# The output product of a state-space branch: weights split on GpSimd, all eight units in three passes, and a norm placed between its matmuls

## The chip, the cores and the metric

The kernel runs on one core of one Trainium2 chip. A core has five engines, each with its own instruction order: TensorE (PE, matmuls; PEld is its weight load), VectorE (DVE), ScalarE (ACT), GpSimd (POOL) and SyncE (SP, which here issues all loads). They share the on-chip memory SBUF; matmuls write to the banks of PSUM, which GpSimd does not read in this kernel. The metric is the device time of one execution in microseconds, lower is better.

## The reference

Two transformer-like blocks over 256 tokens of width 1024. The change lies in the first one:

```
v   = silu(layer_norm(causal_dwconv(a * sigmoid(g), 31 taps)))   # convolution branch
y_a = v @ w_conv_out
y_b = ssd_branch(...) ; its end:  yn @ w_ssm_out                  # state-space branch, yn 256 x 2048
mix = (sigmoid(gate_a) * y_a + sigmoid(gate_b) * y_b) @ w_o
```

Everything is fp32. Behind the block come a feed-forward layer and a second block with two kinds of attention and 32 experts of which all weights (201 MB) are read.

## The kernel before

**Units and passes.** Weights come in units of 128 x 2048 floats (1 MB, one load each) into a ring of five slots. A unit can be multiplied in two ways. In `MODES` with 4, it goes to TensorE as fp32 (two records per matmul in the trace). Otherwise it is split into a high part `wh` (ScalarE copies it to a rounded type, line 260) and a low part `wl` (what is missing, a subtraction on VectorE, line 261), the activation likewise, and three rounded matmuls per block replace the fp32 one: high x high, high x low, low x high. The split goes by halves of 128x1024; four slots hold `wh` and four `wl`, so a half can be split when TensorE has done with the half four before it.

**Around the change.** `ynT` is the state-space branch's normalised result, channels on partitions; `w_ssm_out` comes in eight units `ws0` to `ws7` of 128 output channels each, and two units share a PSUM bank. `ws0` to `ws3` go in fp32, `ws4` to `ws7` in three passes, with their low parts made on VectorE. `gate_gb` takes the product, scaled, from each bank (line 798).

**The convolution branch** is computed on VectorE by taps (line 665): `cacc = vpad * weight + cacc` on 128x256, 30 for each of eight channel blocks after a first multiplication (line 663). 60 of them and ten more, with two first ones, are still to do when `ws0` starts. Then comes the layer norm over channels: `pair_cs` sums blocks in pairs on VectorE; TensorE sums over partitions by a matmul with ones (`cs`, line 820); VectorE centres (line 823); ScalarE squares into `vpad` (line 825); `pair_cq` and `cq` (line 831) sum the squares; `crs` is the reciprocal root, of which the power is a GpSimd operation (line 249); `crr` (line 836) spreads it to all partitions; VectorE multiplies (line 840), ScalarE applies silu and the parts `cT_ah` and `cT_al` feed the next product with `w_conv_out` (`wc0` to `wc3`, `ps_wc`).

**The order.** The program is written in one order, and a planner with its own costs for each instruction decides how the instructions of different steps stand on each engine; `tc.issue_after(x)` holds back a step until `x` stands in the order. On the chip each engine follows its own order and waits on semaphores.

GpSimd's work before is small: eight multiplications `xh` (line 708) in the state-space core, and the powers.

Of the kernel before, what the change touches and what calls it, by code (L numbers as in the profile page):

```python
# [11 lines left out]
F32 = mybir.dt.float32  # L12
# [4 lines left out]
AF = mybir.ActivationFunctionType  # L17
ALU = mybir.AluOpType
# [16 lines left out]
LN_EPS = 1e-5  # L35
# [154 lines left out]
def block_kernel(ctx, tc, I, out, modes):  # L190
    nc = tc.nc
    V, S, G, PE = nc.vector, nc.scalar, nc.gpsimd, nc.tensor
# [4 lines left out]
    mm = ctx.enter_context(tc.tile_pool(name="mm", bufs=4, space=PSUM))  # L197
    sm = ctx.enter_context(tc.tile_pool(name="sm", bufs=2, space=PSUM))
# [9 lines left out]
    def bank(pool, name):  # L208
        return pool.tile([P, 512], F32, tag="b", name=name)
# [17 lines left out]
    ident = const.tile([P, P], F32, name="ident")  # L227
# [4 lines left out]
    def par(name, i=0, n=1):  # L232
        second, o = PPO[name]
        return (pp2 if second else pp)[:, o + i:o + i + n]

    def row(name, pool):
# [2 lines left out]
        nc.sync.dma_start(r, I["rows"][i:i + 1, :].to_broadcast([P, D]))  # L239
        return r  # L240

    def rsqrt(out, in_, scale, eps):

        n = out.free_size()
        first = V.tensor_scalar(out, in_, scale, eps, op0=ALU.mult, op1=ALU.add).ins
        e = neghalf[:, :n]
        if len(out.shape) == 3:
            e = e.rearrange("p (a b) -> p a b", a=out.shape[1])
        G.tensor_tensor(out, out, e, op=ALU.pow)
        return first  # L250


# [3 lines left out]
    sg_pool = dense.enter_context(tc.tile_pool(name="sg", bufs=2, reuse_waits="tile"))  # L256
    ada_pool = sg_pool

    def split(h, l, f):
        a = S.activation(h, f, AF.Copy)  # L260
        return a.ins, V.tensor_tensor(l, f, h.bitcast(F32), op=ALU.subtract).ins  # L261

    def split_act(a, kt, step=4):
        for k in range(0, kt, step):
# [3 lines left out]
    def act(pool, kt, name, tags=("ah", "al"), f=None):  # L268

        return Act(f, *(pool.tile([P, kt, T], F32R, tag=t, name=f"{name}_{t}") for t in tags))  # L270

    def passes(w, name):

        if name in ready:
            return ready.pop(name)[1]
        kt, n = w.shape[1], w.shape[2]
        if mode_of(name) == 4:
            return [(range(kt), range(n), [("f", w)])]
        if kt * n <= HALF:
            cuts = [(range(kt), range(n))]  # L280
        elif "_" in name or n == P:
            cuts = [(range(k, k + kt // 2), range(n)) for k in (0, kt // 2)]
        else:
            cuts = [(range(kt), range(c, c + n // 2)) for c in (0, n // 2)]
        got = []
        for i, (ks, cs) in enumerate(cuts):
            h, l = (hl.tile([P, HALF], F32R, tag=t, name=f"{t}_{name}_{i}")[:, :len(ks) * len(cs)]
                    .rearrange("p (k n) -> p k n", k=len(ks)) for t in ("wh", "wl"))
            split(h, l, w[:, ks[0]:ks[-1] + 1, cs[0]:cs[-1] + 1])
            got.append((ks, cs, [("h", h), ("l", h), ("h", l)]))  # L290
        return got

# [15 lines left out]
        w, _ = stream(name)  # L308
        ready[name] = (w, passes(w, name))

    def gemm_chan(names, x, pool=mm):

        c, banks = 0, []
        for name in names:
            w, _ = stream(name)
            ps_ = passes(w, name)
            for i in range(w.shape[2] // P):
                if c % 2 == 0:
                    banks.append(bank(pool, f"ps_{name}_{i}").rearrange("p (c t) -> p c t", c=2))
                o = banks[-1][:, c % 2, :]  # L320
                c += 1
                m = order(ps_, i * P, P)
                for j, (k, part, wp) in enumerate(m):
                    PE.matmul(o, wp, getattr(x, part)[:, k, :],  # L324
                              start=(j == 0), stop=(j == len(m) - 1))
        return banks

    def gemm_tok(name, x, ktot, pool=mm, early=0):
# [199 lines left out]
    with ExitStack() as e1:  # L528
        b1 = e1.enter_context(tc.tile_pool(name="b1", bufs=1, reuse_waits="tile"))
        hT = act(b1, 8, "hT")  # L530
        vpad = b1.tile([P, 8, T + CK - 1], F32, tag="vpad", name="vpad")
        cacc = b1.tile([P, 8, T], F32, tag="cacc", name="cacc")
        ynT = Act(b1.tile([P, 16, T], F32, tag="ynT", name="ynT"))
        gate = {n: b1.tile([P, 8, T], F32, name=f"gate_{n}") for n in ("ga", "gb")}
# [5 lines left out]
        with tc.tile_pool(name="pre", bufs=1, reuse_waits="tile") as pre:  # L540
# [60 lines left out]
            m = [(k, w, x) for k in range(8) for w, x in ((wd[0], hT.h), (wd[0], hT.l), (wd[1], hT.h))]  # L601
# [29 lines left out]
            for i in range(2):  # L631
                q = rs[:, RSO[f"lambda_q{i + 1}_2"]:RSO[f"lambda_q{i + 1}_2"] + 64]
                k = rs[:, RSO[f"lambda_k{i + 1}_2"]:RSO[f"lambda_k{i + 1}_2"] + 64]
# [156 lines left out]
        late = e1.enter_context(tc.tile_pool(name="late", bufs=1, reuse_waits="tile"))  # L790
# [4 lines left out]
        def ssm_out(j):
            (ps_,) = gemm_chan([f"ws{2 * j}", f"ws{2 * j + 1}"], ynT)
            gt = gate["gb"][:, 2 * j:2 * j + 2, :]
            V.scalar_tensor_tensor(gt, gt, 1.0, ps_, op0=ALU.add, op1=ALU.mult)

        for j in range(WSJ):  # L800
            ssm_out(j)
        for j in range(0, 8, 2):
            for k in range(CK):
                for i in (j, j + 1):
# [12 lines left out]
        pair = pair_sums(cacc, "cs")
        b = bank(sm, "cs")
        for i in range(2):
            PE.matmul(b[:, :T], ones, pair[:, i, :], start=(i == 0), stop=(i == 1))  # L820
        csq = vpad[:, :, :T]
        for i in range(0, 8, 2):
            V.scalar_tensor_tensor(cacc[:, i:i + 2, :], b[:, None, :T].to_broadcast(both), -1.0 / D, cacc[:, i:i + 2, :],
                                   op0=ALU.mult, op1=ALU.add)
            S.activation(csq[:, i:i + 2, :], cacc[:, i:i + 2, :], AF.Square)

        pair = pair_sums(csq, "cq")
        b = bank(sm, "cq")
        for t in range(2):
            for i in range(2):  # L830
                PE.matmul(b[:, t:t + 1], pair[:, i, t * P:(t + 1) * P], ones[:, 0:1], start=(i == 0), stop=(i == 1))
        crs = late.tile([P, 2], F32, name="crs")
        rsqrt(crs, b[:, 0:2], 1.0 / D, LN_EPS)
        b = bank(sm, "crr")
        for t in range(2):
            PE.matmul(b[:, t * P:(t + 1) * P], crs[:, t:t + 1].to_broadcast([P, P]), ident, start=True, stop=True)
        rrow = b[:, None, :T].to_broadcast(both)
        cT = act(b1, 8, "cT", f=cacc)
        for i in range(0, 8, 2):
            V.tensor_tensor(cacc[:, i:i + 2, :], cacc[:, i:i + 2, :], rrow, op=ALU.mult)  # L840
            for c in range(i, i + 2):
                S.activation(cacc[:, c, :], cacc[:, c, :], AF.Silu, scale=par("conv_ln_g", c), bias=par("conv_ln_b", c))
            cT.last = split(cT.h[:, i:i + 2], cT.l[:, i:i + 2], cacc[:, i:i + 2])[1]
        for j in range(WSJ, 4):
            ssm_out(j)
# [4 lines left out]
        mixhl = b1.tile([P, 16, T], F32R, tag="ynT", name="mixhl")  # L850
        mixT = Act(gate["ga"], mixhl[:, :8], mixhl[:, 8:])
        for j in range(4):
            (ps_,) = gemm_chan([f"wc{j}"], cT)
            gt = gate["ga"][:, 2 * j:2 * j + 2, :]
            V.scalar_tensor_tensor(gt, gt, 1.0, ps_, op0=ALU.add, op1=ALU.mult)
            V.tensor_tensor(gt, gt, gate["gb"][:, 2 * j:2 * j + 2, :], op=ALU.add)
            split(mixT.h[:, 2 * j:2 * j + 2], mixT.l[:, 2 * j:2 * j + 2], gt)
        for n in range(2):
            with tc.issue_after(cT.last):
                end = ada_v(n)  # L860
            for t, ps_ in enumerate(gemm_tok(f"wo{n}", mixT, 8, early=2 * n)):
                o = res[:, t, n * 512:(n + 1) * 512]
# [6 lines left out]
    with ExitStack() as e2:  # L869
        b2 = e2.enter_context(tc.tile_pool(name="b2", bufs=1, reuse_waits="tile"))  # L870
        xn1 = b2.tile([P, 2, D], F32, tag="xn1", name="xn1")
        first, last = (norm_rows(xn1, res, t, "ln1", "ln", 4 * LN_EPS) for t in range(2))
# [14 lines left out]
        for j in range(11):  # L887
            banks = gemm_chan([f"up{j}a0", f"up{j}g0"], h1T)
# [49 lines left out]
    with ExitStack() as e3:  # L938
# [7 lines left out]
        ones = dcon.tile([P, P], F32, name="ones2")  # L946
# [121 lines left out]
        for i in range(4):  # L1068
# [458 lines left out]

WSJ = 1  # L1530
# [15 lines left out]
```

## Time and profile before

| | |
|---|---|
| median of 3 runs | 1241.27 us (1239.9 to 2015.82) |
| the profiled execution | 1243.86 us, its span 1242.2 us |
| busy: TensorE, VectorE | 1201.1 us (97%), 776.2 us (62%) |
| busy: ScalarE, GpSimd | 495.3 us (40%), 26.1 us (2%) |
| moved by loads | 353.03 MB, 284 GB/s on average |

A share of busy time is a mean over stages with different limits. A matmul record is longer than its place in the pipe (consecutive ones overlap), so for TensorE the distances between starts count, not the durations.

### The profile page before, as it was taken

The numbers are of one execution on the slowest core, as the hardware profiler recorded it, in microseconds if no ns is written. First come the engines' busy times: TensorE is split into PE (matmuls) and PEld (weight loads), VectorE is DVE, ScalarE is ACT, GpSimd is POOL, SyncE is SP. The second block draws the span as 40 slices with busy tenths as digits, with TensorE's granted clock in tenths as the row PEclk, the third lists the DMA queues.
The fourth block names the chain that finished last, engine by engine and source line by source line (L and its number), as shares of the span: only waits on it lengthen the run. The fifth ranks groups of instructions, "written<-read, shape, count | busy, mean of one in ns | idle before, by whom it ended". The sixth has DMA issues, their size and how long they took to land. (4 is left out here: it accounts for less than half of the span.)

```text
span 1242.2 us, 19480 instructions
## 1 busy us (share of the span) xinstructions
PE 1201.1 (97%) x7885; PEld 881.1 (71%) x7885; DVE 776.2 (62%) x1515; ACT 495.3 (40%) x823; POOL 26.1 (2%) x39
## 2 busy tenths in 40 slices
PE   7999999999999999999999999999999999999886
PEld 6988998998969999875888898554444454444342
DVE  7999999999868989568777656523222223222222
ACT  6456778744426666434445544311111111111111
POOL 0000100100000000001000000000000000000000
PEclk9999999999999999999999989999999999999999
DMA  9635333235867656755883357899999999999995
GB/s 364 234 137 203 128 145 137 103 105 200 355 260 266 237 199 223 274 209 186 331 351 135 104 193 317 328 410 418 419 419 419 420 419 419 419 419 419 418 418 207
DMA packets 51917, 353.03 MB, mean 284 GB/s; under 512 B 6000, under 2 KB 6640, under 8 KB 10224
## 3 DMA queue, kind: packets, MB, share of 16 engines
q1 hardware_dynamic: 51824, 351.75, 72.2%
q8 instruction: 63, 1.03, 0.3%
q14 instruction: 30, 0.25, 0.1%
HBM read 350.68 MB, written 1.05 MB: 283 GB/s over the span
## 5 line engine op out<-in xcount | busy, mean ns | idle before, releaser
L1435 DVE TENSOR_TENSOR hid<-hid,pu 128x256 f32<-128x256 f32 x32 | 12.0, 418 | 195.3 <-PE pu L1427 195.3
L1427 PE MATMUL pu<-we,xg 128*64 128x512 f32 x512 | 117.3, 593 | 6.4 <-DMA we<-in_experts 6.4
L1483 PE MATMUL pd<-we,hdT 128*64 128x512 f32 x512 | 114.0, 595 | 3.8 <-issue 2.6
L1427 PE MATMUL pg<-we,xg 128*64 128x512 f32 x512 | 114.5, 593 | 0.0
L665 DVE SCALAR_TENSOR_TENSOR cacc<-vpad,pp,cacc 128x256 f32<-128x256 f32 x240 | 101.4, 478 | 0.0
L1427 PEld LDWEIGHTS pu<-we,xg 128*64 128x64 f32 x512 | 37.8, 137 | 82.3 <-issue 68.2
L1427 PEld LDWEIGHTS pg<-we,xg 128*64 128x64 f32 x512 | 38.8, 137 | 72.4 <-issue 67.8
L1483 PEld LDWEIGHTS pd<-we,hdT 128*64 128x64 f32 x512 | 35.5, 137 | 70.9 <-issue 68.9
L260 ACT ACTIVATE osb<-ob 128x512 fp32r<-128x512 f32 x31 | 19.6, 631 | 123.4 <-DVE ob L1487 123.4
L1447 ACT ACTIVATE hdT<-ht 128x512 f32<-128x512 f32 x16 | 9.6, 597 | 148.0 <-PE ht L1446 148.0
L1251 DVE TENSOR_SCALAR xg<-xg,s,mod 128x128 f32<-128x128 f32 x64 | 22.0, 404 | 63.7 <-PE xg L1229 63.7
L1487 DVE SCALAR_TENSOR_TENSOR ob<-pd,wpl,g 128x512 f32<-128x512 f32 x31 | 23.3, 751 | 40.3 <-PE pd L1483 37.7
L1430 ACT ACTIVATE hid<-pg 128x512 f32<-128x512 f32 x16 | 9.6, 597 | 84.0 <-PE pg L1427 84.0
L488 DVE SCALAR_TENSOR_TENSOR sb_ada<-w_ada,silu_c,sb_ada 128x512 f32<-128x512 f32 x49 | 36.6, 747 | 0.6
L261 DVE TENSOR_TENSOR wl_dn<-w_dn,wh_dn 128x1024 fp32r<-128x1024 f32 x21 | 25.7, 1224 | 16.6 <-ACT wh_dn L260 16.4
L1229 PE MATMUL xg<-oh,res 128*128 128x128 bf16 (+1 forms) x512 | 35.4, 222 | 0.0
L261 DVE TENSOR_TENSOR obl<-ob,osb 128x512 fp32r<-128x512 f32 x31 | 21.5, 693 | 21.6 <-ACT osb L260 21.6
L260 ACT ACTIVATE wh_dn<-w_dn 128x1024 fp32r<-128x1024 f32 x21 | 22.3, 1061 | 31.5 <-PE ps_dn L335 27.6
L335 PE MATMUL ps_dn<-wh_dn,guT_gh 128*128 128x512 f32 x84 | 33.7, 401 | 0.0
L335 PE MATMUL ps_dn<-wh_dn,guT_gl 128*128 128x512 f32 x84 | 33.2, 395 | 0.0
L324 PE MATMUL ps_xs<-hT_al,wh_xs 128*128 128x256 f32 x128 | 32.2, 287 | 0.0
L324 PE MATMUL ps_xs<-hT_ah,wh_xs 128*128 128x256 f32 x128 | 31.4, 281 | 0.0
(853 smaller groups left out, 3209.9 us busy)
## 6 DMA issues: line engine op xcount, KB each, us to landing
we<-in_experts SPq DMA_DIRECT2D x189, 1024.0 KB, 19.9
w_ada<-in_stream SPq DMA_DIRECT2D x22, 1024.0 KB, 6.4
w_dn<-in_stream SPq DMA_DIRECT2D x10, 1024.0 KB, 4.9
w_xs<-in_stream SPq DMA_DIRECT2D x8, 1024.0 KB, 4.8
w_z<-in_stream SPq DMA_DIRECT2D x8, 1024.0 KB, 4.8
w_ws<-in_stream SPq DMA_DIRECT2D x8, 1024.0 KB, 4.8
w_bc<-in_stream SPq DMA_DIRECT2D x4, 1024.0 KB, 4.8
w_ga<-in_stream SPq DMA_DIRECT2D x4, 1024.0 KB, 5.0
```

The source lines that it names most:

```text
L260: a = S.activation(h, f, AF.Copy)
L261: return a.ins, V.tensor_tensor(l, f, h.bitcast(F32), op=ALU.subtract).ins
L324: PE.matmul(o, wp, getattr(x, part)[:, k, :], start=(j == 0), stop=(j == len(m) - 1))
L335: PE.matmul(banks[t], getattr(x, p_)[:, u + k, t * P:(t + 1) * P], wp, start=(u == 0 and j == 0), stop=(u + kt == ktot and j == len(m) - 1))
L488: V.scalar_tensor_tensor(a, w[:, q, :], c, a, op0=ALU.mult, op1=ALU.add)
L665: V.scalar_tensor_tensor(o, vpad[:, i, k:k + T], par("conv_dw_w", i * CK + k), o, op0=ALU.mult, op1=ALU.add)
L1229: m = PE.matmul(xb[h][:, k * P:(k + 1) * P], x(t, 4 * h + k), oh[:, t].rearrange("p e c -> p (e c)"), start=(i == t == k == 0), stop=(i == ...
L1251: V.tensor_scalar(xg[:, k, :], src, s2[:, k:k + 1], mod[:, 24 + k:25 + k], op0=ALU.mult, op1=ALU.add)
L1427: m = PE.matmul(pgu[i // 2][64 * e:64 * e + 64, :], xg[:, 4 * (i % 2) + k, 64 * e:64 * e + 64], w[i][e][:, k, :], start=(i % 2 == 0 and k ...
L1435: V.tensor_tensor(hd[:, c], hd[:, c], pgu[1][:, c], op=ALU.mult)
L1483: m = PE.matmul(pd[64 * e:64 * e + 64, :], hdT[:, f, 64 * e:64 * e + 64], w[4 + h][e][:, f, :], start=(f == 0), stop=(f == 3))
L1487: V.scalar_tensor_tensor(o[:, c], pd[:, c], wpl, g2[:, h, c], op0=ALU.mult, op1=ALU.mult)
```

## The change

- `ws0` to `ws3` leave `MODES`: all eight units are split and go in three passes.
- The low parts of all eight (`ON_G`) are subtracted on GpSimd, not on VectorE.
- The norm of the convolution branch is cut into three steps and written between the matmuls of the output product: `cs` after the first half of `ws4`, `cq` after 28 matmuls of `ws5`, `crr` after the first matmul of `ws6`. Each is tied to the matmul before it, and the next matmul to it, so that TensorE's order is fixed there.
- The splits of `ws6` and `ws7` come behind the power of `crs` and behind the squares.
- The four gates of `gate_gb` come behind the last `cT_al`, and so do the splits of `wc`.

```diff
-        G.tensor_tensor(out, out, e, op=ALU.pow)
+        powers.append(G.tensor_tensor(out, out, e, op=ALU.pow).ins)
...
-    def split(h, l, f):
+    def split(h, l, f, eng=V):
         a = S.activation(h, f, AF.Copy)
-        return a.ins, V.tensor_tensor(l, f, h.bitcast(F32), op=ALU.subtract).ins
+        return a.ins, eng.tensor_tensor(l, f, h.bitcast(F32), op=ALU.subtract).ins
...
-            split(h, l, w[:, ks[0]:ks[-1] + 1, cs[0]:cs[-1] + 1])
+            split(h, l, w[:, ks[0]:ks[-1] + 1, cs[0]:cs[-1] + 1], G if name in ON_G else V)
...
                 for j, (k, part, wp) in enumerate(m):
-                    PE.matmul(o, wp, getattr(x, part)[:, k, :],
-                              start=(j == 0), stop=(j == len(m) - 1))
+                    if (c - 1, j) in between:
+                        with after(last):
+                            put = between[c - 1, j]()
+                    with after(put):
+                        last = PE.matmul(o, wp, getattr(x, part)[:, k, :],
+                                         start=(j == 0), stop=(j == len(m) - 1)).ins
...
-        for j in range(WSJ):
-            ssm_out(j)
+        pws = [ssm_out(j) for j in range(2)]
...
+        pws.append(ssm_out(2, {(0, 24): center, (1, 28): deviation}))
+
+        with tc.issue_after(powers[-1]), tc.issue_after(squared_c[0]):
+            pws.append(ssm_out(3, {(0, 1): scaled}))
+
+        def ssm_gate(j):
+            gt = gate["gb"][:, 2 * j:2 * j + 2, :]
+            with tc.issue_after(cT.last):
+                V.scalar_tensor_tensor(gt, gt, 1.0, pws[j], op0=ALU.add, op1=ALU.mult)
+
+        for j in range(3):
+            ssm_gate(j)
...
-            (ps_,) = gemm_chan([f"wc{j}"], cT)
+            with tc.issue_after(cT.last):
+                (ps_,) = gemm_chan([f"wc{j}"], cT)
+            if j == 0:
+                ssm_gate(3)
...
-WSJ = 1
-MODES = {n: 4 for n in ("ws0", "ws1", "ws2", "ws3", "wo1_1", "dn1_5", "qm_1", "glu0a0")}
+ON_G = tuple(f"ws{j}" for j in range(8))
+MODES = {n: 4 for n in ("wo1_1", "dn1_5", "qm_1", "glu0a0")}
```

**VectorE, from the last part of `ynT_l` to the centring.** Before:

```order
L261 TENSOR_TENSOR ynT_l<-ynT,ynT_h 128x1024 x3
L665 SCALAR_TENSOR_TENSOR cacc<-vpad,pp,cacc 128x256 x10
L663 TENSOR_SCALAR cacc<-vpad,pp 128x256 x2
L665 SCALAR_TENSOR_TENSOR cacc<-vpad,pp,cacc 128x256 x40
L798 SCALAR_TENSOR_TENSOR gate_gb<-gate_gb,ps_ws_0_2969 128x512
L665 SCALAR_TENSOR_TENSOR cacc<-vpad,pp,cacc 128x256 x20
L810 TENSOR_TENSOR pair_cs<-cacc 128x512
L261 TENSOR_TENSOR wl_ws_0_3346<-w_ws_3343,wh_ws_0_3345 128x1024
L812 TENSOR_TENSOR pair_cs<-pair_cs,cacc 128x512
L261 TENSOR_TENSOR wl_ws_1_3350<-w_ws_3343,wh_ws_1_3349 128x1024
L812 TENSOR_TENSOR pair_cs<-pair_cs,cacc 128x512
```

and in the changed kernel:

```order
L263 TENSOR_TENSOR ynT_l<-ynT,ynT_h 128x1024 x3
L672 SCALAR_TENSOR_TENSOR cacc<-vpad,pp,cacc 128x256 x10
L670 TENSOR_SCALAR cacc<-vpad,pp 128x256 x2
L672 SCALAR_TENSOR_TENSOR cacc<-vpad,pp,cacc 128x256 x60
L814 TENSOR_TENSOR pair_cs<-cacc 128x512
L816 TENSOR_TENSOR pair_cs<-pair_cs,cacc 128x512 x2
L832 SCALAR_TENSOR_TENSOR cacc<-cs,cacc 128x512 x4
```

The gate and the `wl_ws` subtractions are gone from this place; taps and sums now stand in one row.

**GpSimd, from the last power of the state-space core to that of the convolution branch.** Before, `crs` was the next instruction. Now:

```order
L251 TENSOR_TENSOR gr_2452<-gr_2452,neghalf 128x1
L263 TENSOR_TENSOR wl_ws_0_2970<-w_ws_2967,wh_ws_0_2969 128x1024
L263 TENSOR_TENSOR wl_ws_1_2974<-w_ws_2967,wh_ws_1_2973 128x1024
...
L263 TENSOR_TENSOR wl_ws_0_3533<-w_ws_3530,wh_ws_0_3532 128x1024
L263 TENSOR_TENSOR wl_ws_1_3537<-w_ws_3530,wh_ws_1_3536 128x1024
L251 TENSOR_TENSOR crs<-crs,neghalf 128x2
L263 TENSOR_TENSOR wl_ws_0_3598<-w_ws_3595,wh_ws_0_3597 128x1024
L263 TENSOR_TENSOR wl_ws_1_3602<-w_ws_3595,wh_ws_1_3601 128x1024
```

Twelve subtractions (the halves of `ws0` to `ws5`) stand ahead of the power of `crs`, and four (`ws6`, `ws7`) behind it.

**TensorE, around the first product of the norm.** Before, `cs` stood among the last fp32 matmuls of `ws3`:

```order
L324 MATMUL ps_ws_0_3307<-ynT,w_ws_3305 128x256 x16
L324 MATMUL ps_ws_0_3307<-ynT,w_ws_3324 128x256 x13
L820 MATMUL cs<-pair_cs,ones 128x256 x2
L324 MATMUL ps_ws_0_3307<-ynT,w_ws_3324 128x256 x3
L324 MATMUL ps_ws_0_3353<-ynT_h,wh_ws_0_3345 128x256
```

and now behind the first half of `ws4`, at whose end it is tied:

```order
L331 MATMUL ps_ws_0_3466<-ynT_l,wh_ws_0_3458 128x256
L331 MATMUL ps_ws_0_3466<-ynT_h,wl_ws_0_3459 128x256 x8
L830 MATMUL cs<-pair_cs,ones 128x256 x2
L331 MATMUL ps_ws_0_3466<-ynT_h,wh_ws_1_3462 128x256
L331 MATMUL ps_ws_0_3466<-ynT_l,wh_ws_1_3462 128x256
```

It moved from behind the 61st of 64 fp32 matmuls to behind the ninth of sixteen halves.

## Rows read from the trace of the kernel before

**Rows 1.** Page, part 2: GB/s moved in each of 40 equal slices of the span.

```profile
GB/s 364 234 137 203 128 145 137 103 105 200 355 260 266 237 199 223 274 209 186 331 351 135 104 193 317 328 410 418 419 419 419 420 419 419 419 419 419 418 418 207
```

**Rows 2.** Load queue in time: start us, us, queue, line, load, count.

```profile
736.44 161.24 SPq L523 DMA_DIRECT2D we<-in_experts  x64
```

**Rows 3.** Table by stretches: length, busy us (instructions) per engine, granted clock, DMA.

```profile
260.00:270.00 10.00, 10.00 (x66) 9.33 (x66) 10.00 (x27) 2.61 (x3) 0.00 (x0) 1.00 0.01 2
```

**Rows 4.** TensorE in time: start us, us, line, out<-in, count [idle before <-releaser].

```profile
264.37 26.49 PE L324 MATMUL ps_ws<-ynT,w_ws 128*128 128x256 f32 x122
292.21 1.13 PE L820 MATMUL cs<-pair_cs,ones 128*128 128x256 f32 x4 [1.35 <-DVE pair_cs L812]
293.17 1.46 PE L324 MATMUL ps_ws<-ynT,w_ws 128*128 128x256 f32 x6
301.75 0.61 PE L836 MATMUL crr<-ident,crs 128*128 128x128 f32 x4
307.17 0.28 PE L324 MATMUL ps_ws<-ynT_h,wh_ws 128*128 128x256 f32 x1
310.00 0.28 PE L324 MATMUL ps_ws<-ynT_h,wh_ws 128*128 128x256 f32 x1
318.52 0.28 PE L324 MATMUL ps_wc<-cT_ah,wh_wc 128*128 128x256 f32 x1
```

**Rows 5.** VectorE in time, from the taps to the last part of `cT`.

```profile
259.02 4.04 DVE L665 SCALAR_TENSOR_TENSOR cacc<-vpad,pp,cacc 128x256 f32<-128x256 f32 x10
279.47 0.68 DVE L798 SCALAR_TENSOR_TENSOR gate_gb<-gate_gb,ps_ws 128x512 f32<-128x512 f32 x1
280.07 8.00 DVE L665 SCALAR_TENSOR_TENSOR cacc<-vpad,pp,cacc 128x256 f32<-128x256 f32 x20
287.99 0.69 DVE L810 TENSOR_TENSOR pair_cs<-cacc 128x512 f32<-128x512 f32 x1
288.59 1.22 DVE L261 TENSOR_TENSOR wl_ws<-w_ws,wh_ws 128x1024 fp32r<-128x1024 f32 x1
310.91 0.68 DVE L261 TENSOR_TENSOR cT_al<-cacc,cT_ah 128x512 fp32r<-128x512 f32 x1
```

**Rows 6.** GpSimd and ScalarE: two multiplications in time, a group of copies, the squares.

```profile
125.08 2.05 POOL L708 TENSOR_TENSOR xh<-xh,rs 128x512 f32<-128x512 f32 x2 [105.55 <-ACT xh L704]
...
L260 ACT ACTIVATE wh_ws<-w_ws 128x1024 fp32r<-128x1024 f32 x8 | 8.2, 1054 | 15.4 <-DMA w_ws<-in_stream 13.5 <-PE ps_ws L324 1.8
...
294.10 2.43 ACT L825 ACTIVATE vpad<-cacc 128x512 f32<-128x512 f32 x4 [15.79 <-DVE cacc L823]
```

**Rows 7.** GpSimd and VectorE at 224 us, and line 757 elsewhere.

```profile
224.51 0.69 DVE L705 TENSOR_TENSOR xd<-xt,dt 128x512 f32<-128x512 f32 x1
224.55 1.05 POOL L708 TENSOR_TENSOR xh<-xh,rs 128x512 f32<-128x512 f32 x1 [4.02 <-ACT xh L704]
225.12 1.03 DVE L757 TENSOR_TENSOR yg<-yg,zs 128x512 f32<-128x512 f32 x1
...
246.04 0.68 DVE L757 TENSOR_TENSOR yg<-yg,zs 128x512 f32<-128x512 f32 x1
```

**Rows 8.** A power on GpSimd beside VectorE's taps, and one beside another step.

```profile
142.98 0.87 DVE L665 SCALAR_TENSOR_TENSOR cacc<-vpad,pp,cacc 128x256 f32<-128x256 f32 x2
143.15 0.72 POOL L249 TENSOR_TENSOR gr<-gr,neghalf 128x1 f32<-128x1 f32 x1 [16.02 <-DVE gr L245]
...
150.13 0.47 DVE L672 SCALAR_TENSOR_TENSOR bcT<-ps_bc,pp,bcT 128x255 f32<-128x255 f32 x1
150.29 0.56 POOL L249 TENSOR_TENSOR gr<-gr,neghalf 128x1 f32<-128x1 f32 x1 [6.43 <-DVE gr L245]
```

**Rows 9.** TensorE's granted clock in a stretch, and eight transposes, early and later.

```profile
738.00:740.00 2.00, 2.00 (x11) 2.00 (x11) 0.00 (x0) 0.00 (x0) 0.00 (x0) 0.50 0.86 352
...
9.04 1.97 PE L359 MATMUL tr_h<-ident,xn 128*128 128x128 f32 x8 [9.04 <-ACT xn L395]
369.93 1.09 PE L359 MATMUL tr_h<-ident,xn 128*128 128x128 f32 x8
```

More of the change, by code (lines that the diff above doesn't have):

```diff
@@ L240, in row @@
         return r
+    powers = []
     def rsqrt(out, in_, scale, eps):
@@ L309, in prepare, with gemm_chan @@
         ready[name] = (w, passes(w, name))
-    def gemm_chan(names, x, pool=mm):
-        c, banks = 0, []
+    def gemm_chan(names, x, pool=mm, between={}):
+        c, banks, put = 0, [], None
         for name in names:
@@ L793, in block_kernel, with ssm_out @@
         split_act(ynT, 16)
[L795 to L798, printed above, removed]
-        for j in range(WSJ):
-            ssm_out(j)
+        def ssm_out(j, between={}):
+            return gemm_chan([f"ws{2 * j}", f"ws{2 * j + 1}"], ynT, between=between)[0]
+        pws = [ssm_out(j) for j in range(2)]
         for j in range(0, 8, 2):
@@ L815, in block_kernel @@
         both = [P, 2, T]
[L817 to L820, printed above, removed]
         csq = vpad[:, :, :T]
[L822 to L825, printed above, removed]
@@ L827, in block_kernel @@
-        pair = pair_sums(csq, "cq")
-        b = bank(sm, "cq")
-        for t in range(2):
-            for i in range(2):
[L831 to L845, printed above, removed]
+        crs = late.tile([P, 2], F32, name="crs")
@@ new lines, in block_kernel, with center @@
+        cT = act(b1, 8, "cT", f=cacc)
+        pair_c = pair_sums(cacc, "cs")
+        pair_q, squared_c = [], []
+        def center():
+            b = bank(sm, "cs")
+            for i in range(2):
+                m = PE.matmul(b[:, :T], ones, pair_c[:, i, :], start=(i == 0), stop=(i == 1)).ins
+            for i in range(0, 8, 2):
+                V.scalar_tensor_tensor(cacc[:, i:i + 2, :], b[:, None, :T].to_broadcast(both), -1.0 / D, cacc[:, i:i + 2, :],
+                                       op0=ALU.mult, op1=ALU.add)
+                squared_c[:] = [S.activation(csq[:, i:i + 2, :], cacc[:, i:i + 2, :], AF.Square).ins]
+            pair_q.append(pair_sums(csq, "cq"))
+            return m
@@ new lines, in deviation, with scaled @@
+        def deviation():
+            b = bank(sm, "cq")
+            for t in range(2):
+                for i in range(2):
+                    m = PE.matmul(b[:, t:t + 1], pair_q[0][:, i, t * P:(t + 1) * P], ones[:, 0:1], start=(i == 0), stop=(i == 1)).ins
+            rsqrt(crs, b[:, 0:2], 1.0 / D, LN_EPS)
+            return m
+        def scaled():
+            b = bank(sm, "crr")
+            for t in range(2):
+                m = PE.matmul(b[:, t * P:(t + 1) * P], crs[:, t:t + 1].to_broadcast([P, P]), ident, start=True, stop=True).ins
+            rrow = b[:, None, :T].to_broadcast(both)
+            for i in range(0, 8, 2):
+                V.tensor_tensor(cacc[:, i:i + 2, :], cacc[:, i:i + 2, :], rrow, op=ALU.mult)
+                for c in range(i, i + 2):
+                    S.activation(cacc[:, c, :], cacc[:, c, :], AF.Silu, scale=par("conv_ln_g", c), bias=par("conv_ln_b", c))
+                cT.last = split(cT.h[:, i:i + 2], cT.l[:, i:i + 2], cacc[:, i:i + 2])[1]
+            return m
```

## The prediction

> **What bounds the kernel now.** I read the slices of the page first: from about slice 26 on the core moves some 418 GB/s without a break [rows 1]. That is the expert stage, fed by loads whose unbroken issue starts only at 736.4 us [rows 2], when the dense stages have left their buffers. What delays the dense stages delays that start and the end alike, so a microsecond at 300 us is taken as one at the end. The table by stretches comes second: at 260 to 270 us both TensorE and VectorE are busy for 10.0 of 10 us, and GpSimd for none [rows 3]. Two engines are full at once there: a change that takes work from one must not put it on the other.
>
> Third, TensorE's order in time [rows 4]. The output product runs from 264.37 to 318.52 us, where the convolution branch's product takes over: 54.15 us. Units 0 to 3 in fp32 are 64 matmuls, two records each: 122 records in 26.49 us and 6 in 1.46, so 27.95 us. A half of a split unit (24 matmuls) goes from 307.17 to 310.00: 2.83 us. The only wait is 1.35 us for `pair_cs`. Fourth, VectorE [rows 5]: from 259.02 to 287.99 us it does 72 taps with one gate between them, then the sums. It is the side that decides when `cs` can run.
>
> **The passes.** In three passes units 0 to 3 take 8 halves x 2.83 = 22.64 us in place of 27.95: -5.3. The three small products of the norm stay what they are and cancel. If the `pair_cs` wait goes too, the stretch is 54.15 - 5.31 - 1.35 = 47.5 us.
>
> **VectorE without GpSimd.** It loses the gate ahead of the sums (0.60 us, 279.47 to 280.07) and the eight weight subtractions that stood between and behind the sums. Taps would end at 287.99 - 0.60 = 287.4; three sums at 0.60 (287.99 to 288.59), the last 0.69, end at 289.3. TensorE reaches the fixed place of `cs` after nine halves, at 264.37 + 9 x 2.83 = 289.84. On paper the place fits.
>
> **GpSimd's sixteen subtractions.** No row shows a 128x1024 subtraction there. Two 128x512 operations with two inputs took 2.05 us back to back [rows 6], so I take 2.0 for one, between 1.84 (twice a hold of 0.92, below) and 2.1 (twice 1.05). ScalarE's copy ahead is 1.05 us [rows 6], 16 instead of 8, in time where it is idle. A split can start when TensorE leaves the half four before it, and is needed 3 x 2.83 + 1.9 = 10.4 us later; copy and subtraction are 3.1, so TensorE need not wait for weights.
>
> **What they do to the taps** is the step that decides. A GpSimd operation with two inputs began at 224.55 and lasted 1.05; a VectorE multiply of two SBUF tensors issued at 225.12 then took 1.03 us where the same line takes 0.68 elsewhere [rows 7]. Ending at 226.15, it had its inputs from about 225.47: GpSimd had held it off for 0.92 us from its own start. The multiply whose first input is in PSUM kept its 0.69 beside it. A tap reads `vpad` and `cacc`, both in SBUF. The small power on GpSimd says that a tap takes part in this: beside a step of the small convolution, which reads PSUM, it takes 0.56 us; beside taps 0.72 [rows 8]. Two taps still took 0.87, so GpSimd got in at the next boundary between taps and the one-element power held them up by nothing visible. A 1024-element operation will.
>
> The Trainium skill says the same as a rule (SBUF — State Buffer, section "Who interferes with whom"): a VectorE instruction with two SBUF inputs contends with a GpSimd instruction that reads SBUF, and the loser waits for the whole instruction. By it the taps wait in full, and rows 7 agree for a multiply (0.35 us); no row shows a tap behind a long GpSimd operation.
>
> So GpSimd's time is added to VectorE's. Twelve subtractions (units 0 to 5) stand ahead of `crs` in GpSimd's queue; each is released by 288 us as TensorE frees a half, so all fall among the taps. 12 x 2.0 = 24.0 us, and about 0.08 for each restart of the taps (0.48 alone against 0.40 in a row): 25.0. `pair_cs` ends near 314.3, and `cs`, at a fixed place, holds every later product on TensorE: a wait of 314.3 - 289.84 = 24.5 us. Bounds: 12 x 1.84 = 22.1 and 12 x 2.18 = 26.2.
>
> The skill's page GPSIMD Engine Reference, section "Performance versus the Vector engine", gives 4497 ns for a two-input add of 2048 elements; half is an estimate of 2.25 us, and the sum by it would be 3 us longer. The 512-element rows are nearer, and are used.
>
> **Behind the wait.** After a thin stretch TensorE ran at a granted 0.50, 1.2 GHz (738 to 740 us), and after the idle start of the program eight transposes took 1.97 us against 1.09 later [rows 9]. After 24 us of waiting I expect half speed for about 4 us: +2, between 0 and 3.4. From `cs` to `cq` TensorE has 52 matmuls, 6.1 us; the squares end 294.10 + 2.43 - 292.21 = 4.3 us after `cs` [rows 4, 6], one sum behind them at 5.0: covered. From `crr` to the last `cT_al` it was 311.6 - 301.75 = 9.9 us [rows 4, 5]; TensorE now has 95 matmuls there, 11.2 us, so the first `wc` product finds its data with 1 us to spare, less if the last four subtractions hold up `cT_al`. Without that cover: up to 2 us more, kept in the upper end. The weights' loads start earlier, since GpSimd frees ring slots before TensorE has read them; nothing waits for them there.
>
> **Sum.** The stretch becomes 47.5 + 24.5 + 2 = 74.0 us against 54.15: +19.8. The profiled execution took 1243.86 us, 2.6 over the median 1241.27; on the median this is **1261 us**, +1.6%. With the lower bounds (22.1, no restarts, no slow clock) it is 47.5 + 21.6 - 54.15 = +14.9, 1256; with the upper (26.2 and 1.0, 3.4, 2.0) +24.5, 1266: 47.5 + 25.7 + 3.4 + 2 - 54.15.
>
> **Rivals.**
> - Taps go on beside GpSimd. For it: two taps in 0.87 us beside the power [rows 8]. Against: the 1.03 us of rows 7. Then 47.5 - 54.15 = -6.7: 1235 us, faster than before. It decides where all twelve subtractions together hold VectorE by less than 0.5 + 6.7 = 7.2 us, 0.6 each. Chance 0.13.
> - VectorE wins the port and GpSimd waits until the taps end. TensorE then stops at the first missing low part, 264.37 + 2.83 + 1.9 = 269.1, until some 291.4 and runs on unhindered: 22.3 us of waiting, less the 6.7, and 2 for the clock: 1259. Against: the power came in between taps. Chance 0.08.
> - The third: GpSimd is slower on this form, 2.6 us and more for 1024 elements. Then 12 x 2.68 = 32.2 and the end is 7 us later, 1268; at 3 us, 1273. Above 2.4 us each the loss passes 2%. For: no row has this size or output type. Chance 0.13.
> - The forecast: 0.66.
>
> That the edit does not take effect is no case: the order shows three passes for all eight units.
>
> **Numbers.** Two per cent, 24.8 us, is about what a measurement of this kernel can tell from no change. Faster by more: 0.01, since even the first rival gives 0.5%. Slower by more: 0.11 of the third rival and 0.05 of the forecast, whose upper end touches the bound: 0.16. Within: 0.83. The range leaves out the first rival and the end of the third, and takes in a part-way case where taps are held for two thirds of the time (-8 us on the forecast): 1248 to 1270.
>
> **What would show it.** Right: taps in the stretch 260 to 310 that last 2 us and more, GpSimd busy some 24 us there, one wait of TensorE of 22 to 27 us at `cs` behind `pair_cs`, a granted clock under 1 behind it, and the first `ps_wc` near 338. Wrong: taps all at 0.48 and `cs` near 290 (first rival); TensorE waiting for `wl_ws` (second); `wl_ws` over 2.4 us (third).

## The result and the profile after

The changed kernel takes 1262.05 us (median of 6 runs, 1256.25 to 1262.2) against 1239.98 us for the kernel before on the same chip: a ratio of 1.016, 95% interval 1.0135 to 1.0184. It is 22 us slower, which lies within the two per cent; the prediction was 1261 us, with a range of 1248 to 1270. The ratios in this document are formed from the fast executions, without one of the kernel before that took 2015.82 us, and not from the medians (these would give 1.018). The profiled execution is the shortest of the six: 1256.25 us, span 1254.5.

First GpSimd in time (start us, us), where nothing answered before:

```profile
258.15 29.03 POOL L263 TENSOR_TENSOR wl_ws<-w_ws,wh_ws 128x1024 fp32r<-128x1024 f32 x11 [9.41 <-ACT wh_ws L262]
287.55 2.44 POOL L263 TENSOR_TENSOR wl_ws<-w_ws,wh_ws 128x1024 fp32r<-128x1024 f32 x1 [0.37 <-ACT wh_ws L262]
325.70 0.70 POOL L251 TENSOR_TENSOR crs<-crs,neghalf 128x2 f32<-128x2 f32 x1 [35.71 <-DVE crs L247]
326.37 9.60 POOL L263 TENSOR_TENSOR wl_ws<-w_ws,wh_ws 128x1024 fp32r<-128x1024 f32 x4
```

Twelve subtractions run before `crs`, as forecast. Eleven in a row take 2.64 us each; the four behind `crs`, where VectorE has no taps, take 2.40. VectorE at the same time, to be held against [rows 5]:

```profile
259.04 25.85 DVE L672 SCALAR_TENSOR_TENSOR cacc<-vpad,pp,cacc 128x256 f32<-128x256 f32 x10
284.81 2.84 DVE L670 TENSOR_SCALAR cacc<-vpad,pp 128x256 f32<-128x256 f32 x2
287.58 26.05 DVE L672 SCALAR_TENSOR_TENSOR cacc<-vpad,pp,cacc 128x256 f32<-128x256 f32 x60
313.56 0.68 DVE L814 TENSOR_TENSOR pair_cs<-cacc 128x512 f32<-128x512 f32 x1
314.27 1.42 DVE L816 TENSOR_TENSOR pair_cs<-pair_cs,cacc 128x512 f32<-128x512 f32 x2
317.86 2.48 DVE L832 SCALAR_TENSOR_TENSOR cacc<-cs,cacc 128x512 f32<-128x512 f32 x4 [2.17 <-PE cs L830]
```

Ten taps took 4.04 us before; here they take 25.85, and the last 60, most of them without GpSimd, 26.05. The view of the tile `cacc` alone gives nine of them apart, from 262 to 285 us (minimum/median/maximum of one in ns):

```profile
L672 DVE SCALAR_TENSOR_TENSOR cacc<-vpad,pp,cacc x9: 2645/2652/2658, 261.6 to 282.2; 128x256 f32<-128x256 f32 x9
```

So while both engines stand in a row, exactly one tap passes per GpSimd subtraction, in step with it. VectorE counts as busy for the whole time that a tap waits: in the table below it reads 26.00 of 26. TensorE's waits (total, times, longest), and the stretches (length, then busy us of PE, PEld, DVE, ACT, POOL, granted clock, DMA):

```profile
PE cs L830 <- DVE pair_cs L816: 25.6, 1, 25.6
```

```profile
264.00:290.00 26.00, 26.00 (x221) 25.89 (x219) 26.00 (x12) 9.69 (x10) 25.53 (x11) 1.00 0.58 203
290.00:300.00 10.00, 0.09 (x1) 0.00 (x0) 10.00 (x26) 0.00 (x0) 0.00 (x0) 0.76 0.30 106
300.00:310.00 10.00, 0.00 (x0) 0.00 (x0) 10.00 (x27) 0.00 (x0) 0.00 (x0) 0.50 0.00 0
...
315.00:319.00 4.00, 3.26 (x11) 2.90 (x12) 1.83 (x3) 0.42 (x1) 0.00 (x0) 0.50 0.00 0
319.00:322.00 3.00, 3.00 (x27) 3.00 (x27) 2.79 (x6) 3.00 (x6) 0.00 (x0) 0.97 0.00 0
```

TensorE runs out of products at 290 us, stands for 25.6 us, and does its first 3 us behind the wait at 0.50. The chain that ended last shows the two ends of the stretch:

```profile
259.13 25.76 DVE cacc L672 x10
284.89 2.77 DVE cacc L670 x2
287.65 25.98 DVE cacc L672 x60
...
315.74 2.07 PE cs L830 x4
317.82 6.82 PE ps_ws L331 x52
324.64 0.79 PE cq L843 x8
```

The first `ps_wc` comes at 339.53 us instead of 318.52 [rows 4], 21.0 later, and the expert loads begin 20.7 us later than in [rows 2] (TensorE in time, then the load queue):

```profile
339.53 0.28 PE L331 MATMUL ps_wc<-cT_ah,wh_wc 128*128 128x256 f32 x1
...
757.15 478.39 SPq L530 DMA_DIRECT2D we<-in_experts  x196
```

### The profile page after: what moved, and what is told of

Its sections match the earlier page's. It is cut to its first block, busy times and chain, and to the rows that moved or that the text cites. A ratio compares the mean times of both kernels' runs of the same rounds, so it can differ in the third digit from the quotient of the medians.

```text
span 1254.5 us, 19648 instructions
## 1 busy us (share of the span) xinstructions
PE 1192.0 (95%) x7949; PEld 876.1 (70%) x7949; DVE 796.7 (64%) x1507; ACT 503.3 (40%) x831; POOL 67.1 (5%) x55
## 4 chain that ended last, share of the span: by engine, by line
PE 55%; DMA 14%; DVE 7%; ACT 2%; issue 1%; POOL 0%; POOLq 0%; ACTq 0%; SPq 0%; DVEq 0%
DMA we<-in_experts 14%; PE pd L1512 6%; PE pu L1456 5%; PE pg L1456 5%; PE ps_dn L342 5%; DVE cacc L672 4%; PE ps_wo L342 2%; PE ps_wc L331 2%; PE ps_wu L342 2%; PE ps_ws L331 2%; PE acc L1434 2%; PE xg L1258 1%; PE ps_gm L331 1%; ACT xg L441 1%; PE ps_qm L342 1%; PE ps_pd L331 1%
## 5 line engine op out<-in xcount | busy, mean ns | idle before, releaser
L672 DVE SCALAR_TENSOR_TENSOR cacc<-vpad,pp,cacc 128x256 f32<-128x256 f32 x240 | 125.1, 575 | 0.0
L1516 DVE SCALAR_TENSOR_TENSOR ob<-pd,wpl,g 128x512 f32<-128x512 f32 x31 | 23.3, 751 | 37.1 <-PE pd L1512 34.4
L263 POOL TENSOR_TENSOR wl_ws<-w_ws,wh_ws 128x1024 fp32r<-128x1024 f32 x16 | 41.0, 2596 | 9.9 <-ACT wh_ws L262 9.8
L262 ACT ACTIVATE wh_dn<-w_dn 128x1024 fp32r<-128x1024 f32 x21 | 22.3, 1061 | 31.6 <-PE ps_dn L342 24.5
L331 PE MATMUL ps_ws<-ynT_h,wh_ws 128*128 128x256 f32 x128 | 32.2, 289 | 0.0
```

The costliest lines, as they stand in the source:

```text
L263: return a.ins, eng.tensor_tensor(l, f, h.bitcast(F32), op=ALU.subtract).ins
L331: last = PE.matmul(o, wp, getattr(x, part)[:, k, :], start=(j == 0), stop=(j == len(m) - 1)).ins
L672: V.scalar_tensor_tensor(o, vpad[:, i, k:k + T], par("conv_dw_w", i * CK + k), o, op0=ALU.mult, op1=ALU.add)
L1516: V.scalar_tensor_tensor(o[:, c], pd[:, c], wpl, g2[:, h, c], op0=ALU.mult, op1=ALU.mult)
```

## The experiments

Three theories were set against each other. The **port theory** is the forecast's: a GpSimd operation that reads SBUF holds VectorE's taps off, and TensorE waits at `cs` for them. The **place theory**: the fixed places of `cs`, `cq` and `crr` make TensorE wait, whichever engine subtracts. The **any-work theory**: any work on GpSimd beside the taps slows VectorE.

**1. The subtractions on VectorE, all else as in the changed kernel.**

```diff
-ON_G = tuple(f"ws{j}" for j in range(8))
+ON_G = ()
```

> The change, with all sixteen low parts subtracted on VectorE in place of GpSimd; passes and places stay. Port theory (a GpSimd operation that reads SBUF holds off VectorE's operations with two SBUF inputs for as long as it runs): VectorE now pays 1.14 us for each of the ten subtractions ahead of cs, 11.4 us, where GpSimd cost it some 25; the wait at cs falls from 25.6 to about 11 us, taps stay at 0.40 us, the time is 1243 to 1249 us. Rival, place theory (the fixed place of cs and TensorE's fixed order cost the time, whoever subtracts): the wait stays over 20 us and the time near 1262. Rival, any-work theory (VectorE is slowed by any busy GpSimd): as the port theory here.

Measured: 1241.54 us, ratio 1.0015 (0.9992 to 1.0038), a little under the expected 1243. The whole loss in time is gone, with every place where it was: the place theory falls. VectorE, and TensorE's wait:

```profile
278.02 18.72 DVE L672 SCALAR_TENSOR_TENSOR cacc<-vpad,pp,cacc 128x256 f32<-128x256 f32 x47
296.62 0.72 DVE L814 TENSOR_TENSOR pair_cs<-cacc 128x512 f32<-128x512 f32 x1
```

```profile
PE ps_ws L331 <- DVE wl_ws L263: 9.2, 1, 9.2
```

The taps run at 0.40 us apiece again, though VectorE has eight halves more to subtract ahead of the sums. TensorE's wait is not at `cs` now (0.3 us there) but just ahead of it: in the ninth half it stands for the low part, which VectorE subtracts behind the first sum, at 297.22 us. A half that VectorE subtracts itself takes 1.23 us, of which the start of the next instruction overlaps 0.09 (1.14 from start to start); the same half on GpSimd takes 2.2 us of VectorE's time, as the next runs show.

**2. GpSimd writes and reads nothing.** The low parts are filled with zeros, so this kernel leaves them out of the product.

```diff
+        if eng is G:
+            for c in range(2):
+                last = G.memset(l[:, l.shape[1] // 2 * c:l.shape[1] // 2 * (c + 1)].bitcast(F32), 0.0).ins
+            return a.ins, last
```

> The change, with GpSimd writing zeros into each low part (two fills of 128x512) in place of the subtraction: the low parts of the weights are left out of the product. GpSimd is still busy at the same places and writes the same bytes, but reads nothing. Port theory: taps at 0.40 us, wait at cs under 1.5 us, 1233 to 1237 us. Place theory: the wait stays over 15 us, the time over 1250. Any-work theory: taps are slowed in proportion to GpSimd's busy time, at least 10 us at cs, 1245 and more.

Measured: 1230.19 us, ratio 0.9916 (0.9888 to 0.9943), 3 us better than expected. GpSimd (first row) and VectorE (the others):

```profile
256.97 0.99 POOL L265 MEMSET wl_ws<- 128x512 f32 x2 [7.47 <-PE ps_gb L335]
```

```profile
259.80 4.05 DVE L676 SCALAR_TENSOR_TENSOR cacc<-vpad,pp,cacc 128x256 f32<-128x256 f32 x10
263.76 0.73 DVE L674 TENSOR_SCALAR cacc<-vpad,pp 128x256 f32<-128x256 f32 x2
264.41 23.86 DVE L676 SCALAR_TENSOR_TENSOR cacc<-vpad,pp,cacc 128x256 f32<-128x256 f32 x60
288.17 0.70 DVE L818 TENSOR_TENSOR pair_cs<-cacc 128x512 f32<-128x512 f32 x1
```

Twenty fills beside the taps (four of the 24 ahead of `crs` lie outside them) cost them nothing: 259.80 to 288.17 is 28.37 us for the 72, against 28.35 in run 7, where GpSimd does nothing there, and 54.50 in the changed kernel (259.13 to 313.63 in the chain). The any-work theory falls. TensorE waits nowhere between 264 and 345 us, and the first `ps_wc` comes at 312.8. This is what the three passes and the places are worth if the low parts come free. A fill is shorter than a subtraction, so the next run keeps GpSimd as long at work.

**3. GpSimd reads one input.** It multiplies the high part by zero; the low parts are again left out of the product.

```diff
+        if eng is G:
+            return a.ins, G.tensor_scalar(l, h.bitcast(F32), 0.0, None, op0=ALU.mult).ins
```

> The change, with GpSimd multiplying the high part by zero into the low part (one SBUF input, 128x1024) in place of the two-input subtraction: the low parts are left out of the product. Port theory: it reads SBUF, so it holds the taps off for its own time, but that is shorter; at 1.0 to 1.5 us each, twelve cost 12 to 18 us, the wait at cs is 11 to 17 us and the time 1246 to 1255 us. If only two-input GpSimd operations contend: taps at 0.40, 1233 to 1237 us. Place theory: near 1262.

Measured: 1243.59 us, ratio 1.0019 (1.0002 to 1.0037), below the expected 1246. GpSimd and VectorE:

```profile
257.95 34.17 POOL L264 TENSOR_SCALAR wl_ws<-wh_ws 128x1024 fp32r<-128x1024 f32 x12 [9.41 <-ACT wh_ws L262]
```

```profile
258.84 5.60 DVE L674 SCALAR_TENSOR_TENSOR cacc<-vpad,pp,cacc 128x256 f32<-128x256 f32 x10
264.36 1.44 DVE L672 TENSOR_SCALAR cacc<-vpad,pp 128x256 f32<-128x256 f32 x2
265.73 30.88 DVE L674 SCALAR_TENSOR_TENSOR cacc<-vpad,pp,cacc 128x256 f32<-128x256 f32 x60
296.53 0.68 DVE L816 TENSOR_TENSOR pair_cs<-cacc 128x512 f32<-128x512 f32 x1
```

GpSimd is busy for longer than with the subtractions (34.17 us for 12), and VectorE loses far less: 37.69 - 28.37 = 9.3 us, 0.78 for each operation of 2.85. The loss falls on single taps, the others keep their time (minimum/median/maximum in ns):

```profile
L674 DVE SCALAR_TENSOR_TENSOR cacc<-vpad,pp,cacc x70: 470/475/1258, 258.8 to 296.1; 128x256 f32<-128x256 f32 x70
```

By the Trainium skill (SBUF — State Buffer, section "Who interferes with whom") a VectorE instruction with two SBUF inputs contends with a GpSimd instruction that reads SBUF and not with one that only writes; by the section "SBUF: two separate sides" of the same page the loser waits for the whole instruction. The fills agree. For one input the measurement differs in size: the taps wait for about a quarter of the operation, not for all of it. The run changes the kind of operation together with the number of inputs, so that the number decides is not shown apart from that.

**4. More subtractions ahead of the sums, the norm later.** The products of the norm go behind `ws5`, and nothing holds back the splits of `ws6` and `ws7`, so that all sixteen can run among the taps.

```diff
-        pws.append(ssm_out(2, {(0, 24): center, (1, 28): deviation}))
+        pws.append(ssm_out(2))
-        with tc.issue_after(powers[-1]), tc.issue_after(squared_c[0]):
-            pws.append(ssm_out(3, {(0, 1): scaled}))
+        if True:
+            pws.append(ssm_out(3, {(0, 1): center, (0, 46): deviation, (1, 20): scaled}))
```

> The change, with the three products of the norm at later places (cs after the first matmul of ws6, cq near the end of ws6, crr in ws7) and the splits of ws6 and ws7 not held back, so all sixteen GpSimd subtractions come ahead of crs. Port theory: TensorE gets three more halves before cs (8.5 us), but the taps still end late, later by four more GpSimd operations (cs near 325 us), and the rest of the norm then stands behind it: 1260 to 1270 us, no gain. Place theory: the wait at cs shrinks by at least 8 us and the time to 1253 or less.

Measured: 1272.29 us, ratio 1.0237 (1.0201 to 1.0273): the slowest of all, a little over the expected 1270. From its first product to the place of `cs` TensorE has 34.4 us of work (265.4 to 299.8) instead of 25.8, and still waits 25.6 us there, because VectorE is later by as much:

```profile
260.06 25.78 DVE L672 SCALAR_TENSOR_TENSOR cacc<-vpad,pp,cacc 128x256 f32<-128x256 f32 x10
...
288.54 34.68 DVE L672 SCALAR_TENSOR_TENSOR cacc<-vpad,pp,cacc 128x256 f32<-128x256 f32 x60
323.14 0.68 DVE L814 TENSOR_TENSOR pair_cs<-cacc 128x512 f32<-128x512 f32 x1
```

**5. Fewer subtractions.**

```diff
-ON_G = tuple(f"ws{j}" for j in range(8))
+ON_G = tuple(f"ws{j}" for j in range(4))
```

> The changed kernel with only ws0 to ws3 subtracted on GpSimd (8 halves, where the changed kernel has 12 ahead of the sum cs), ws4 to ws7 on VectorE. Port theory (each GpSimd subtraction lets VectorE through with about one tap): VectorE loses 8 x 2.2 = 17 us ahead of cs instead of 12 x 2.2 = 26, and does two of the ws4 halves itself there (2.3 us): cs starts at about 309 us, some 7 us before the changed kernel's, and 1248 to 1254 us. Rival, a queue theory: the loss comes from the length of GpSimd's queue and not from each operation, so that with a third of it gone most of the loss is gone: 1241 to 1245 us.

Measured: 1255.11 us, ratio 1.0091 (1.0052 to 1.013); `cs` starts at 309.7 us. A little over the upper end in time, in place as expected. As in run 1 TensorE stands just ahead of `cs`, for the low part of the ninth half, which VectorE subtracts behind the first sum. The wait, then VectorE:

```profile
PE ps_ws L331 <- DVE wl_ws L263: 17.5, 1, 17.5
...
259.76 21.41 DVE L672 SCALAR_TENSOR_TENSOR cacc<-vpad,pp,cacc 128x256 f32<-128x256 f32 x10
281.10 0.73 DVE L670 TENSOR_SCALAR cacc<-vpad,pp 128x256 f32<-128x256 f32 x2
281.74 23.84 DVE L672 SCALAR_TENSOR_TENSOR cacc<-vpad,pp,cacc 128x256 f32<-128x256 f32 x60
305.49 0.69 DVE L814 TENSOR_TENSOR pair_cs<-cacc 128x512 f32<-128x512 f32 x1
```

The dose decides. From the first of the 72 taps to the first sum, in runs where VectorE does nothing else between:

| GpSimd subtractions among the taps | 72 taps take, us | over 28.37, for each |
|---|---|---|
| 0 (run 2; run 7: 28.35) | 28.37 | |
| 8 (run 5) | 45.73 | 2.17 |
| 12 (the changed kernel) | 54.50 | 2.18 |
| 16 (run 4) | 63.08 | 2.17 |

A queue theory, by which a shorter queue would lose most of the loss, falls.

**6. The three passes alone**, in the kernel before: `ws0` to `ws3` leave `MODES`, nothing on GpSimd, the planner's order.

```diff
-MODES = {n: 4 for n in ("ws0", "ws1", "ws2", "ws3", "wo1_1", "dn1_5", "qm_1", "glu0a0")}
+MODES = {n: 4 for n in ("wo1_1", "dn1_5", "qm_1", "glu0a0")}
```

> The kernel before with ws0 to ws3 split on VectorE and multiplied in three passes like ws4 to ws7; nothing on GpSimd, no fixed places. The passes save TensorE 5.3 us of the stretch; the 8 subtractions cost VectorE 8 x 1.14 = 9.1 us among the taps, so pair_cs ends near 297 instead of 288 us. Port theory: that is all, and the time is that of the experiment with everything on VectorE, 1238 to 1246 us, with a wait of 5 to 9 us before cs. Rival (the fixed places are worth something by themselves): slower than that experiment by 3 us or more, over 1245 us.

Measured: 1251.96 us, ratio 1.0072 (1.005 to 1.0093): outside the expected range, on the rival's side. TensorE's longest wait, and VectorE around its end:

```profile
PE ps_ws L324 <- DVE wl_ws L261: 16.6, 1, 16.6
```

```profile
265.20 1.23 DVE L261 TENSOR_TENSOR wl_ws<-w_ws,wh_ws 128x1024 fp32r<-128x1024 f32 x1
...
277.47 15.15 DVE L665 SCALAR_TENSOR_TENSOR cacc<-vpad,pp,cacc 128x256 f32<-128x256 f32 x38
292.51 0.71 DVE L810 TENSOR_TENSOR pair_cs<-cacc 128x512 f32<-128x512 f32 x1
293.12 1.24 DVE L261 TENSOR_TENSOR wl_ws<-w_ws,wh_ws 128x1024 fp32r<-128x1024 f32 x1
```

My count assumed eight subtractions among the taps. In this order there are four; the fifth stands behind the first sum, at 293.12, and TensorE waits for it while the taps run. In run 1, with the same passes, all eight stand ahead of the last 47 taps. So what the changed program's order is worth beside the passes is some 10 us (1251.96 against 1241.54, with 1240.35 and 1240.92 for the kernel before beside them). Whether the fixed places give it or the order in which the units and the taps are written was not taken apart.

**7. The places alone**: `ws0` to `ws3` back in fp32, nothing on GpSimd.

```diff
-ON_G = tuple(f"ws{j}" for j in range(8))
+ON_G = ()
-MODES = {n: 4 for n in ("wo1_1", "dn1_5", "qm_1", "glu0a0")}
+MODES = {n: 4 for n in ("ws0", "ws1", "ws2", "ws3", "wo1_1", "dn1_5", "qm_1", "glu0a0")}
```

> The kernel after's fixed places alone: ws0 to ws3 stay in single fp32 products and ws4 to ws7 are split on VectorE, as in the kernel before; cs, cq and crr stand at the fixed places. Nothing runs on GpSimd among the taps. Port theory: VectorE's taps end near 288 us, nothing waits long for them, and the places move a few small products: 1238 to 1243 us. Place theory (the places themselves make TensorE wait): 1246 us or more.

Measured: 1242.01 us, ratio 0.999 (0.9966 to 1.0013): no difference. TensorE does not wait at `cs` any more (busy 81.0 of 81 us from 264 to 345), and the first `ps_wc` comes at 317.6.

**8. and 9. Between: two or one of these units in three passes**, with the places, all on VectorE, as candidates for a kernel faster than both. Their edit is that of run 7, with `ws0` and `ws1`, or `ws0` to `ws2`, in `MODES`.

> The changed kernel with every subtraction on VectorE and ws0 and ws1 back in single fp32 products: four subtractions less among the taps (4 x 1.14 = 4.6 us of VectorE) for 2.65 us more of TensorE. pair_cs then ends near 296 us instead of 300.7, TensorE runs out of products near 293 instead of 290, and its idle stretch shrinks from 10 us to 2 or 3. By the port theory (VectorE's time ahead of cs is what counts) 1233 to 1239 us, faster than both kernels by a little; if the stretch is bounded by all of VectorE's work up to the first ps_wc (75 of 81 us busy) rather than by the work ahead of cs: 1239 to 1243 us.

> The fixed places with everything on VectorE, ws0 to ws2 in single fp32 products and ws3 alone in three passes: a candidate for a kernel faster than both. Beside the run with the places alone, TensorE saves 1.33 us and VectorE does 2 more subtractions (2.3 us) among the taps: pair_cs ends near 294.5 us, the place of cs is reached near 294.2, so TensorE waits less than 1 us and the first ps_wc comes near 316.5 us. If an earlier first ps_wc is worth as much at the end, 1238 to 1240 us where the kernel before has 1240.4, a gain of at most 0.3%; if something behind the dense stages gives it back (as the run with the places alone may show: first ps_wc 0.9 us earlier, same time), 1240 to 1243 us.

Measured: with two, 1242.93 us, ratio 0.9991 (0.9966 to 1.0015), waits of 2.2 us for `wl_ws` and 1.1 at `cs`, first `ps_wc` at 320.2; with one, 1241.38 us, ratio 1.0008 (0.999 to 1.0026), next to no wait, first `ps_wc` at 317.2. The waits are as expected, the gain is not there: both times lie in the second of the two ranges that were expected. None of the kernels that compute the whole product beats the kernel before.

## Why the prediction was right

- **The passes (-5.3) and the place of `cs`.** TensorE was at the place at 290.1 us (315.74 - 25.6), forecast 289.84. Run 2 gives the whole stretch without a hold: from 265.14 to 312.78 us, 47.6, forecast 47.5.
- **GpSimd's time is added to VectorE's.** Right, and the step that decides: runs 1 to 5. Forecast 25.0 us for the twelve, measured 54.50 - 28.37 = 26.1. Of [rows 7] only the held multiply bears on it: the one with an input in PSUM had begun at 224.51, ahead of GpSimd's operation at 224.55, and shows nothing of a hold.
- **The size of one subtraction.** Too small: 2.0 us forecast, 2.40 measured without taps and 2.64 among them; two operations of 512 elements took 2.05 [rows 6], one of 1024 with another output type takes more than both. That the loss was still only 2.18 each has a second reason that I had not seen: one tap of 0.40 passes within each 2.64. The two errors nearly cancel, and that is luck. The estimate of 2.25 from the Trainium skill's page GPSIMD Engine Reference (section "Performance versus the Vector engine") was nearer to the 2.40 than my 2.0.
- **The wait at `cs`.** Forecast 24.5, measured 25.6: the sums ended at 315.7, 1.4 us later than forecast, and TensorE came to the place 0.3 later.
- **Half speed behind the wait (+2).** From `cs` to `cq` it takes 315.74 to 324.64, 8.9 us; in run 2, at full clock, from 290.7 to 297.7, 7.0. So +1.9. The 4 us of half speed behind it were not worked out from a row; here it was 0.50 from 315.7 to 319 us. Of [rows 9] only the first shows a lower clock: from 9 to 11 us, where the eight transposes are slow, the granted clock reads 1.00.
- **The cover at `wc`.** It held, by 1.2 us: the last `cT_al` ends at 338.33, TensorE comes to `wc` at 339.53. The last four subtractions did hold up `cT_al`, as the forecast had left open: from `cacc<-cacc,crr` to the last `cT_al` it takes 9.8 us (328.49 to 338.33) against 8.7 in run 2 (301.73 to 310.46). The rows stand in the last section.
- **The sum.** The stretch to the first `ps_wc` grew by 21.0 us, forecast 19.8, and the medians by 22.1. (The forecast's upper end names 1.0 us for the restarts beside the 26.2, which has them in it already, 12 x 2.18; its 1266 counts them once.) The profiled execution by itself grew by 12.4 us only (1256.25 against 1243.86), though its expert loads were 20.7 late. The two profiles differ behind that point in the granted clock: 0.83 in one stretch around the start of the expert loads before (last section), 1.00 there after:

```profile
750.00:800.00 50.00, 48.51 (x327) 44.53 (x327) 31.69 (x52) 19.82 (x34) 3.06 (x3) 1.00 0.83 322
```

That the clock makes the difference in time is not shown. The step "a microsecond at 300 us is one at the end" fits this pair of medians, but it is no rule: by the table in the last section the first 5.8 of the 21.0 us cost next to nothing (run 1), and the other 15.2 cost some 21. That the two come out at 22.1 together is luck too.
- **The rivals.** Taps going on freely beside GpSimd: excluded by the nine taps of 2.65 us. VectorE winning: excluded, TensorE never waited for `wl_ws`. The slower GpSimd: its condition came true (2.64 us), its price did not (2.68 of VectorE for each), because of the tap that passes.

## What to carry to other kernels

Before moving elementwise work from VectorE to GpSimd, look at what VectorE does meanwhile and where its operands lie. Beside the taps, instructions with two SBUF inputs, a two-input GpSimd operation took more of VectorE's time (2.17 us) than the work that it took away (1.14 to 1.23 us). And where a small product is put at a fixed place in TensorE's order, everything behind it pays for a late operand.

## What was not expected of the hardware

**One tap passes per GpSimd operation.** I had reckoned with VectorE held for the whole queue or slowed evenly. Nine taps in a row lasted 2645 to 2658 ns, with one for each subtraction. And the hold depends on what GpSimd reads: nothing for a fill, 0.78 us for an operation of 2.85 with one input, 2.17 for one of 2.64 with two. These runs show who waits and for how long; what the two engines share is not seen in a trace.

**It is no fixed turn, and it is not only the taps.** Three more VectorE rows of the changed kernel stand beside GpSimd's subtractions, the first among the first twelve, the others beside the last four (326.37 to 335.97 us):

```profile
L670 DVE TENSOR_SCALAR cacc<-vpad,pp x1: 2518/2518/2518, 284.8 to 284.8; 128x256 f32<-128x256 f32 x1
...
328.49 2.48 DVE L854 TENSOR_TENSOR cacc<-cacc,crr 128x512 f32<-128x512 f32 x4 [2.87 <-PE crr L851]
331.56 4.96 DVE L263 TENSOR_TENSOR cT_al<-cacc,cT_ah 128x512 fp32r<-128x512 f32 x1 [0.59 <-ACT cT_ah L262]
```

The first multiplication of a channel block, with one tensor from SBUF and its parameters, took 2518 ns where it takes 0.41 us in run 2, so it was held too. The four multiplications with `crr`, one input of which lies in PSUM, took 2.48 us as in run 2: not held. And `cT_al`, with both inputs in SBUF, took 4.96 us where it takes 0.69 in run 2: it had its inputs at 331.56 and ended only at 336.5, behind the last subtraction, so it did not pass at the boundary between the last two, at some 333.6. What decides who goes first at a boundary stays open.

**The last few microseconds don't come through.** First `ps_wc` and median time of all kernels:

| kernel | first `ps_wc` at, us | median, us |
|---|---|---|
| run 2, fills | 312.8 | 1230.19 |
| run 9, one unit | 317.2 | 1241.38 |
| run 7, places alone | 317.6 | 1242.01 |
| before | 318.5 | 1239.98 to 1240.92 |
| run 8, two units | 320.2 | 1242.93 |
| run 3, one input | 322.8 | 1243.59 |
| run 1, on VectorE | 324.3 | 1241.54 |
| run 6, passes alone | 332.8 | 1251.96 |
| run 5, eight | 333.5 | 1255.11 |
| after, twelve | 339.5 | 1262.05 |
| run 4, sixteen | 349.1 | 1272.29 |

The place is read from one profiled execution of each kernel, and the output product itself starts between 264.4 and 265.4 us in them. From 324 us on, 25 us at that point are 31 at the end; between 317 and 324 next to nothing comes through. In the profiled executions the granted clock is low at different places: from 730 to 750 us it is 0.83 in the kernel before and in run 7 and 1.00 in runs 1, 3, 8 and 9, and from 1215 to 1240 us it is 0.96 and 0.93 in the former and 0.76 to 0.91 in the latter. The stretches around the start of the expert loads and at the end, of the kernel before, then of run 9:

```profile
730.00:750.00 20.00, 18.51 (x133) 18.39 (x132) 10.12 (x16) 7.07 (x13) 1.65 (x1) 0.83 0.67 260
...
1215.00:1240.00 25.00, 16.35 (x72) 7.34 (x68) 6.97 (x16) 5.21 (x12) 1.10 (x2) 0.96 0.51 185
```

```profile
730.00:750.00 20.00, 18.50 (x153) 18.17 (x153) 13.54 (x21) 9.24 (x12) 1.65 (x1) 1.00 0.75 286
...
1215.00:1240.00 25.00, 11.71 (x44) 5.12 (x44) 6.00 (x14) 4.77 (x12) 1.10 (x2) 0.76 0.30 113
```

Run 9 keeps full speed at 730 us, issues its last expert load 6 us earlier (734.86 + 478.75 = 1213.6, before 736.44 + 483.22 = 1219.7), and ends only 2.6 us earlier (spans of 1239.6 and 1242.2 us), at a mean clock of 0.76 in the last 25 us. That the clock takes the rest is not shown: one execution of each doesn't make a rule, and run 2 kept full speed at 730 us and gained to the end. What grants the clock in these stretches stays open, and with it why the kernels of the plateau agree.
